# Matrix product with RMS norm on one core: roots of finished row blocks in one batch, second row factor and transpose earlier, last head copy ahead of sums

## The chip, the cores and the metric

The kernel runs on one core of a Trainium2 chip. The metric is the device time of one execution in microseconds (us), lower is better. Executions of one kernel mostly agree within 0.3%. TensorE (PE) multiplies matrices, VectorE (DVE) and ScalarE (ACT) work on elements, GpSimd (POOL) and SyncE (SP) issue transfers (DMA). A line number such as L279 is a line of the kernel. The changed kernel has more lines, so the same statement has another number there; both are given where it matters.

## The reference

```python
m, k, n = 2048, 2048, 2048          # a, b: float32, drawn from a normal distribution
x = np.matmul(a, b)
rms = np.sqrt(np.mean(x ** 2, axis=-1, keepdims=True) + eps)
return (gamma * x / rms).astype(np.float32)
```

## The kernel before

Rows of `a` are handled in 16 blocks of 128. The first four blocks (the head) are multiplied directly while `b` streams in. Blocks 4 to 15 go in pairs, called groups 2 to 7. Each group is computed in two halves of the columns, and each half with seven products of sums of quarters, in the manner of Strassen, instead of eight plain products. A product is eight 128x512 matmuls into one PSUM bank; products 4 and 3 add onto the banks of products 2 and 5, once those have been copied away or used.

A row block must be made ready for its group: ACT takes its norm (two squares and a root, `row_norm`), DVE makes a power of two of it (`row_factor`), ACT scales the block to fp16 (`row_apply`, L231), and a DMA transposes it (L186). DVE then forms sums of its quarters (`a_sums`, tiles s_103 to s_107). When a pair of rows is done, `finish` takes the root of the mean square, inverts it and multiplies the rows by it and by gamma.

```python
    def transpose_half(mb, g):
        bank = ps_t.tile([P, CH], FP32, name="tbank")
        view = bank.bitcast(FP16).rearrange("p (g m) -> p g m", m=P)
        for n in range(8):
            kt = g * 8 + n
            nc.tensor.matmul(
                view[:, n, :], a16[mb][:, kt * P:(kt + 1) * P], identity_h,
                is_transpose=True, start=(n == 0), stop=(n == 7),
            )
        nc.vector.tensor_copy(out=at(mb)[:, g * 8:(g + 1) * 8, :], in_=view)

    def transpose_dma(mb):
        nc.sync.dma_start_transpose(at(mb), a16[mb])
...
    def row_norm(mb):

        n2 = stat_pool.tile([P, 2], FP32, name="n2")
        for h in range(2):
            junk = sq_pool.tile([P, 2 * CH], BF16, name="sq")
            nc.scalar.activation(out=junk, in_=a32[mb][:, h * HALF:(h + 1) * HALF],
                                 func=ACTF.Square, scale=2.0 ** -8, accum_out=n2[:, h:h + 1])
        norm[mb] = stat_pool.tile([P, 1], FP32, name="norm")
        nc.scalar.activation(out=norm[mb], in_=n2[:, 0:1], func=ACTF.Sqrt, bias=n2[:, 1:2],
                             scale=1.0)

    def row_factor(mb):
        s = stat_pool.tile([P, 1], FP32, name="s")
        nc.vector.tensor_scalar_max(out=s, in0=norm.pop(mb), scalar1=1e-18)
        nc.vector.reciprocal(out=s, in_=s)
        nc.vector.tensor_single_scalar(out=s.bitcast(I32), in_=s.bitcast(I32),
                                       scalar=0x7F800000, op=ALU.bitwise_and)
        new_msq(mb)
        nc.vector.tensor_scalar(out=msq[mb][:, NCH:], in0=s, scalar1=s, scalar2=float(eps),
                                op0=ALU.mult, op1=ALU.mult)
        factor[mb] = s

    def row_apply(mb):
        a16[mb] = a16_slot(mb)
        if mb < HB + 2:
            nc.vector.tensor_scalar_mul(out=a16[mb], in0=a32.pop(mb), scalar1=factor.pop(mb))
        else:
            nc.scalar.activation(out=a16[mb], in_=a32.pop(mb), func=ACTF.Copy,
                                 scale=factor.pop(mb))
...
    def inverse_rms(last, partial=None):

        rms = stat_pool.tile([P, 1], FP32, name="rms")
        if partial is None:
            tot = stat_pool.tile([P, 1], FP32, name="tot")
            nc.vector.reduce_sum(out=tot, in_=msq.pop(last), axis=mybir.AxisListType.X)
            nc.scalar.activation(out=rms, in_=tot, func=ACTF.Sqrt)
        else:
            nc.scalar.activation(out=rms, in_=last, func=ACTF.Sqrt, bias=partial, scale=1.0)
        r = stat_pool.tile([P, 1], FP32, name="r")
        nc.vector.reciprocal(out=r, in_=rms)
        return r

    def rows(mb, lo, hi):
        return out[mb * P:(mb + 1) * P, lo:hi]

    def finish(mb, order=(0, 1)):
        r = inverse_rms(mb)
        for h in order:
            x = x_half.pop((mb, h))
            nc.vector.scalar_tensor_tensor(
                out=x, in0=x, scalar=r, in1=gamma_sb[:, h * HALF:(h + 1) * HALF],
                op0=ALU.mult, op1=ALU.mult)
            nc.sync.dma_start(out=rows(mb, h * HALF, (h + 1) * HALF), in_=x)
```

The end of the head, where block 5 (HB + 1) is transposed by TensorE through the one bank of `ps_t`:

```python
    groups2 = [(r, c) for r in range(HB) for c in (2, 3)][:-1]
    for kp in range(KP):
        load_later(1)
        before = [lambda: transpose_half(HB, 0)] if kp == 6 else []
        if kp == 7:
            before = [lambda: transpose_half(HB, 1)]
        stream(groups2, kp, before)
        square(squares[kp][0], x_chunk(*squares[kp]))
        if kp == 4:
            prepare(HB)
        if kp == 6:

            prepare(HB + 1)
        else:
            b_sums_2(min(kp, KP - 2))
...
    evict(groups2[2:-1], ())
    bank = new_bank()
    for kt in range(KT):
        if kt in (0, 6):
            transpose_half(HB + 1, kt // 6)
        head_matmul(bank, r3, 3, kt)
    evict(groups2[-1:], ())
    row_norm(HB + 2)
    a_sums(G0, (2, 5, 1))
    finish(0, (1, 0))
    b_sums_2(KP - 1)
    nc.scalar.copy(out=x_chunk(r3, 3), in_=bank)
    squares2(1)

```

One half of a group, and what is hooked between its products (group G0 is 2, r3 is block 3):

```python
        x11, x12, x21, x22 = (x_chunk(ra, c1), x_chunk(ra, c2), x_chunk(rb, c1), x_chunk(rb, c2))
        t = x22
        at_hook(0)
        p2, p5 = new_bank(), new_bank()
        product(g, j, 2, p2)

        c = spare if (g, j) == (G0, 0) else t
        nc.scalar.copy(out=c, in_=p2)
        last_squares()
        at_hook(1)
        product(g, j, 5, p5)
        nc.vector.tensor_tensor(out=t, in0=p5, in1=c, op=ALU.add)
        at_hook(2)
        p1 = new_bank()
        product(g, j, 1, p1)
        nc.vector.tensor_tensor(out=t, in0=p1, in1=t, op=ALU.subtract)
        at_hook(3)
        product(g, j, 4, p2, start=False)
        nc.scalar.copy(out=x21, in_=p2)
        square(rb, x21)
        nc.vector.tensor_tensor(out=x11, in0=t, in1=x21, op=ALU.add)
        at_hook(4)
        product(g, j, 3, p5, start=False)
        nc.scalar.copy(out=x12, in_=p5)
...
            else:
                if g == G0 + 1:
                    hook(2, finish, r3)
                hook(0, row_factor, nxt)
                hook(1, apply, nxt)
                hook(1, row_norm, nxt + 1)
                hook(3, row_factor, nxt + 1)
                hook(4 if g == G0 + 1 else 3, finish, 2 * g - 2)
                hook(4, apply, nxt + 1)
        else:
            if g == G0:
                hook(1, squares2, r3)
                for kp in range(KP):
                    hook(2, b_sum_6, 1, kp)
            else:
                hook(2, finish, 2 * g - 1)
            if more:
                hook(3, a_sums, g + 1, (2, 5, 1))
                hook(6, a_sums, g + 1, (7,))
                hook(7, a_sums, g + 1, (6,))
            if g + 2 < NG:
                hook(0, load_after, g, nxt + 2)
                hook(0, load_block, nxt + 3)
                hook(5, row_norm, nxt + 2)
```

In the traces here ACT, DVE and SP run their instructions in the order in which the program emits them: in the kernel before, ACT takes the norm of block 9 at 103.01 us and only then, at 103.21, the root of block 3, as the text has them. So a statement's place in this text decides what it can be held up by.

## Time and profile before

| | before |
|---|---|
| time, median of 3 runs | 226.4 us (226.37 to 226.68) |
| span of the profiled execution | 224.8 us |
| TensorE busy / DVE / ACT | 94% / 72% / 58% |
| spacing of 128x512 matmuls, start to start | 216 ns |
| time TensorE lost between 64 us and its last matmul | 0.71 + 0.53 + 1.12 = 2.36 us |

The busy share of TensorE alone says little. The Trainium skill, page "Perfetto Trace Analysis", section "Identifying the Most-Contended Engine", says that matmul busy time is no good measure of the distance to the limit, and section "Optimization Strategy" says to find the gaps of the engine and what each waits for.

These are lines of the waits view of the kernel before, filtered to TensorE. The columns are engine, tile and line, what it waited for, and then us in total, times, and longest.

```profile
PE acc L279 <- DVE s_104 L244: 1.0, 1, 1.0
PE tbank L179 <- DVE at_even L183: 0.5, 1, 0.5
PE acc L279 <- ACT x_102 L484: 0.4, 1, 0.4
```

The timeline of TensorE of the kernel before shows the same three places. The columns are start in us, duration in us, engine, line, operation, output and inputs, shape, count, and in brackets the idle time before it and what ended it.

```profile
66.25 0.59 PE L341 MATMUL acc<-b_2_87,head_at 128*128 128x512 bf16 x2
67.39 0.61 PE L179 MATMUL tbank<-identity_h,x_102 128*128 128x128 f16 x8 [0.55 <-DVE at_even L183]
...
109.70 1.89 PE L279 MATMUL acc<-early,s_103 128*128 128x512 bf16 x8
111.96 3.61 PE L279 MATMUL acc<-early,head_at 128*128 128x512 bf16 x16 [0.36 <-ACT x_102 L484]
...
118.64 0.38 PE L279 MATMUL acc<-b_7_92,s_106 128*128 128x512 bf16 x1
119.98 0.39 PE L279 MATMUL acc<-b_0_77,s_104 128*128 128x512 bf16 x1 [0.96 <-DVE s_104 L244]
```

The idle time in brackets understates the loss. A matmul's record is 0.38 us long, but its successor normally starts after 0.216 us. From start to start, the last wait is 119.98 - 118.64 = 1.34 us instead of 0.22, so 1.12 us are lost. In the same way the other two lose 0.71 and 0.53 us (each 0.16 us more than the bracket).

What stands behind the first wait is seen in DVE's timeline of the kernel before, where the copy that empties the transpose bank (L183, at 66.65) comes after the sums of slice 6 (L269, L254 and L259):

```profile
64.59 0.68 DVE L269 TENSOR_TENSOR b_6_83<-b_6_83 128x1024 bf16<-128x1024 bf16 x1
65.19 1.09 DVE L254 TENSOR_TENSOR early<-b_6_91 128x512 bf16<-128x512 bf16 x3
66.31 0.42 DVE L259 TENSOR_TENSOR b_6_91<-b_6_91 128x512 bf16<-128x512 bf16 x1
66.65 0.68 DVE L183 COPY at_even<-tbank 128x1024 f16<-128x1024 f16 x1
```

The other two waits go back to group 3, which prepares block 9. These are lines of DVE's timeline of the kernel before:

```profile
98.90 0.15 DVE L316 TENSOR_REDUCE tot<-msq 128x1 f32<-128x5 f32 x1
103.43 0.16 DVE L321 RECIPROCAL r<-rms 128x1 f32<-128x1 f32 x1 [4.38 <-ACT rms L317]
103.63 1.28 DVE L331 SCALAR_TENSOR_TENSOR x_98<-x_98,r,gamma_sb 128x1024 f32<-128x1024 f32 x1
...
107.92 0.15 DVE L316 TENSOR_REDUCE tot<-msq 128x1 f32<-128x5 f32 x1
...
119.23 0.69 DVE L244 TENSOR_TENSOR s_104<-at_even 128x1024 f16<-128x1024 f16 x1 [1.96 <-DMA at_even<-head_at]
```

And these are lines of ACT's and of SP's timelines of the kernel before in the same stretch:

```profile
103.01 0.30 ACT L212 ACTIVATE norm<-n_994 128x1 f32<-128x1 f32 x1
103.21 0.19 ACT L317 ACTIVATE rms<-tot 128x1 f32<-128x1 f32 x1
...
108.11 0.20 ACT L317 ACTIVATE rms<-tot 128x1 f32<-128x1 f32 x1 [3.48 <-DVE tot L316]
108.22 1.99 ACT L231 ACTIVATE head_at<-a_867,s 128x2048 f16<-128x2048 f32 x1
...
111.34 0.56 ACT L484 COPY x_102<-acc 128x512 f32<-128x512 f32 x1
```

```profile
111.05 0.33 SPq L334 DMA_DIRECT2D out_dram<-x_96  x1
111.48 3.35 SPq L186 DMA_TRANSPOSE at_even<-head_at  x1
```

Read together: DVE reduced the squares of block 3 at 98.90, then stood for 4.38 us until ACT took the root at 103.21, because that root stands behind the norm of block 9 in ACT's order. The root of block 4 waits 3.48 us for its sum (108.11), the scaling of block 9 stands behind that root (108.22), the copy of product 2 (L484) behind the scaling, and the transpose (111.48) behind the stores of block 4. The transpose lands at 119.2, and TensorE stands for s_104.

### The profile page before, as it was taken

Reading aid. Unit: us, or ns where it says so; the run is one execution under the profiler, and the core shown is the slowest. Engines: PE = TensorE matmul, PEld = TensorE weight load, DVE = VectorE, ACT = ScalarE, POOL = GpSimd, SP = SyncE. Lnnn points to the kernel's source line nnn. Section 1 sums busy time; section 2 is a strip of 40 time slices with the busy share of each in tenths; the row PEclk is TensorE's granted clock in tenths of the full one; section 3 lists DMA queues with packets and bytes.
Section 4 is the critical chain, followed back from the end, with each engine's and each line's share of the span. In section 5 each row is a group of like instructions: output and inputs, shape, how many; then the busy total and the mean of one; then the engine's idle time right before and its main releaser. Section 6 shows DMA issues by size and latency. Waiting matters only on the chain.

```text
span 224.8 us, 3025 instructions
## 1 busy us (share of the span) xinstructions
PE 212.1 (94%) x1043; PEld 98.6 (44%) x1043; DVE 161.8 (72%) x324; ACT 129.4 (58%) x272; POOL 24.5 (11%) x49
## 2 busy tenths in 40 slices
PE   7899999999999999999998999999999999999950
PEld 2445444444444444444443444444444444444430
DVE  1427567983998989965977578957895579687692
ACT  2210003708697895795673987698587874334570
POOL 8524232200000002000020002000200000000000
PEclk9999999999999999999999999999999999999996
DMA  6999999999962499906589369956994694044045
GB/s 190 219 203 209 202 209 210 212 305 284 331 261 117 187 280 280 345 32 169 238 210 391 118 157 241 350 205 169 225 337 187 96 279 187 0 187 191 0 188 187
DMA packets 36176, 47.13 MB, mean 210 GB/s; under 512 B 21952, under 2 KB 26048, under 8 KB 34496
## 3 DMA queue, kind: packets, MB, share of 16 engines
q0 software_dynamic: 9648, 23.33, 41.3%
q1 hardware_dynamic: 26080, 22.29, 32.7%
q10 hardware_dynamic: 432, 1.31, 2.0%
q8 instruction: 8, 0.13, 0.2%
q14 instruction: 8, 0.07, 0.1%
HBM read 34.60 MB, written 16.78 MB: 229 GB/s over the span
## 4 chain that ended last, share of the span: by engine, by line
PE 57%; DMA 14%; issue 12%; DVE 6%; ACT 5%; POOL 3%; DVEq 0%; ACTq 0%; POOLq 0%
PE acc L279 41%; PE acc L341 15%; DMA b_4_81<-in_b_dram 8%; DMA at_even<-head_at 3%; DMA a_865<-in_a_dram 2%; ACT sq L209 2%; ACT sq L291 1%; POOL early L106 1%; ACT head_at L231 1%; PE tbank L373 1%; PE tbank L165 1%; DVE x_95 L331 1%; DVE x_98 L331 1%; DVE x_96 L331 1%; DVE x_102 L331 1%
## 5 line engine op out<-in xcount | busy, mean ns | idle before, releaser
L341 PEld LDWEIGHTS <-head_at 128*128 128x128 bf16 x240 | 22.9, 98 | 26.6 <-issue 1.1
L279 PEld LDWEIGHTS <-s_104 128*128 128x128 f16 x96 | 9.3, 98 | 12.5 <-DVE s_104 L244 1.4
L279 PEld LDWEIGHTS <-head_at 128*128 128x128 f16 x96 | 9.4, 98 | 11.9 <-issue 0.6
L279 PEld LDWEIGHTS <-s_105 128*128 128x128 f16 x96 | 9.4, 98 | 11.3
L279 PEld LDWEIGHTS <-s_103 128*128 128x128 f16 x96 | 9.4, 98 | 11.3
L279 PEld LDWEIGHTS <-at_even 128*128 128x128 f16 x96 | 9.4, 98 | 11.3
L279 PEld LDWEIGHTS <-s_107 128*128 128x128 f16 x96 | 9.4, 98 | 11.3
L384 ACT COPY x_95<-acc 128x512 f32<-128x512 f32 x1 | 0.6, 585 | 23.8 <-PE acc L341 23.8
L279 PEld LDWEIGHTS <-s_106 128*128 128x128 f16 x88 | 8.6, 98 | 10.4
L279 PE MATMUL acc<-t_left,s_103 128*128 128x512 bf16 x48 | 11.3, 379 | 0.0
L279 PE MATMUL acc<-early,s_103 128*128 128x512 bf16 x48 | 11.3, 379 | 0.0
L279 PE MATMUL acc<-early,head_at 128*128 128x512 bf16 x48 | 10.8, 379 | 0.4 <-ACT x_102 L484 0.4
L279 PE MATMUL acc<-early,at_even 128*128 128x512 bf16 x48 | 10.8, 379 | 0.0
L279 PE MATMUL acc<-t_left,at_even 128*128 128x512 bf16 x48 | 10.8, 379 | 0.0
L279 PE MATMUL acc<-t_left,head_at 128*128 128x512 bf16 x48 | 10.8, 379 | 0.0
L379 DVE TENSOR_TENSOR x_98<-tbank,x_98 128x512 f32<-128x512 f32 x7 | 4.8, 692 | 7.6 <-PE tbank L373 7.6
L317 ACT ACTIVATE rms<-tot 128x1 f32<-128x1 f32 x14 | 2.8, 199 | 12.2 <-DVE tot L316 12.2
L217 DVE TENSOR_SCALAR s<-norm 128x1 f32<-128x1 f32 x12 | 1.8, 148 | 10.9 <-ACT norm L212 10.9
L321 DVE RECIPROCAL r<-rms 128x1 f32<-128x1 f32 x16 | 2.6, 164 | 9.5 <-ACT rms L317 8.4
L170 DVE COPY head_at<-tbank 128x1024 bf16<-128x1024 bf16 x7 | 4.8, 692 | 6.2 <-PE tbank L165 6.2
L291 ACT ACTIVATE sq<-x_97 128x512 bf16<-128x512 f32 x8 | 5.0, 628 | 3.5 <-DVE x_97 L599 3.0
L209 ACT ACTIVATE sq<-a_430 128x1024 bf16<-128x1024 f32 x2 | 2.1, 1058 | 7.5 <-DMA a_430<-in_a_dram 7.5
(390 smaller groups left out, 552.6 us busy)
## 6 DMA issues: line engine op xcount, KB each, us to landing
out_dram<-x_99 SPq DMA_DIRECT2D x4, 512.0 KB, 3.5
out_dram<-x_95 SPq DMA_DIRECT2D x4, 512.0 KB, 2.6
out_dram<-x_96 SPq DMA_DIRECT2D x4, 512.0 KB, 3.0
out_dram<-x_100 SPq DMA_DIRECT2D x4, 512.0 KB, 6.0
out_dram<-x_97 SPq DMA_DIRECT2D x4, 512.0 KB, 2.8
out_dram<-x_101 SPq DMA_DIRECT2D x4, 512.0 KB, 3.7
early<-in_a_dram POOLq DMA_DIRECT2D x7, 256.0 KB, 15.2
out_dram<-x_98 SPq DMA_DIRECT2D x3, 512.0 KB, 2.7
```

Source lines behind the costliest of these rows:

```text
L106: nc.gpsimd.dma_start(out=ah(kp), in_=a[0:HB * P, kp * W2:(kp + 1) * W2].rearrange("(r p) k -> p r k", p=P))
L165: nc.tensor.matmul(view[:, t, r, :], ah(kp)[:, r, t * P:(t + 1) * P], identity, is_transpose=True, start=(t == 0 and r == 0), stop=(t == 1 ...
L170: nc.vector.tensor_copy(out=head_at[:, 2 * kp:2 * kp + 2, :, :], in_=view)
L209: nc.scalar.activation(out=junk, in_=a32[mb][:, h * HALF:(h + 1) * HALF], func=ACTF.Square, scale=2.0 ** -8, accum_out=n2[:, h:h + 1])
L231: nc.scalar.activation(out=a16[mb], in_=a32.pop(mb), func=ACTF.Copy, scale=factor.pop(mb))
L279: nc.tensor.matmul(bank, lhsT[:, kp, :], rhs, start=(start and kp == 0), stop=(kp == KP - 1), skip_group_check=not start)
L291: nc.scalar.activation(out=sq[:, 0:CH], in_=src, func=ACTF.Square, scale=inv_sqrt_n, accum_out=msq[mb][:, c:c + 1])
L317: nc.scalar.activation(out=rms, in_=tot, func=ACTF.Sqrt)
L321: nc.vector.reciprocal(out=r, in_=rms)
L331: nc.vector.scalar_tensor_tensor(out=x, in0=x, scalar=r, in1=gamma_sb[:, h * HALF:(h + 1) * HALF], op0=ALU.mult, op1=ALU.mult)
L341: nc.tensor.matmul(bank, head_at[:, kt, r, :], head_rhs(c, kt), start=(kt == 0), stop=(kt == KT - 1))
L379: nc.vector.tensor_tensor(out=x, in0=part, in1=x, op=ALU.add)
```

## The change

It means to shorten these waits by order alone. The roots of all finished blocks are taken in one batch before the next block's norm (`take_rms`); the second row factor comes earlier, meant to let its scaling and transpose start earlier too; and at the end of the head the copy out of the transpose bank goes ahead of the sums of slice 6 (of L254 and L259; those of L269 stay ahead of it). No instruction is added or removed.

```diff
--- before.py
+++ after.py
@@ -308,24 +308,33 @@
     def x_chunk(mb, c):
         return x_tile(mb, c // 2)[:, (c % 2) * CH:(c % 2 + 1) * CH]
 
-    def inverse_rms(last, partial=None):
-
-        rms = stat_pool.tile([P, 1], FP32, name="rms")
-        if partial is None:
-            tot = stat_pool.tile([P, 1], FP32, name="tot")
-            nc.vector.reduce_sum(out=tot, in_=msq.pop(last), axis=mybir.AxisListType.X)
-            nc.scalar.activation(out=rms, in_=tot, func=ACTF.Sqrt)
-        else:
-            nc.scalar.activation(out=rms, in_=last, func=ACTF.Sqrt, bias=partial, scale=1.0)
+    rms_of = {}
+
+    def take_rms(mb):
+
+        tot = stat_pool.tile([P, 1], FP32, name="tot")
+        nc.vector.reduce_sum(out=tot, in_=msq.pop(mb), axis=mybir.AxisListType.X)
+        rms_of[mb] = stat_pool.tile([P, 1], FP32, name="rms")
+        nc.scalar.activation(out=rms_of[mb], in_=tot, func=ACTF.Sqrt)
+
+    def inverse(rms):
         r = stat_pool.tile([P, 1], FP32, name="r")
         nc.vector.reciprocal(out=r, in_=rms)
         return r
 
+    def inverse_rms(last, partial):
+
+        rms = stat_pool.tile([P, 1], FP32, name="rms")
+        nc.scalar.activation(out=rms, in_=last, func=ACTF.Sqrt, bias=partial, scale=1.0)
+        return inverse(rms)
+
     def rows(mb, lo, hi):
         return out[mb * P:(mb + 1) * P, lo:hi]
 
     def finish(mb, order=(0, 1)):
-        r = inverse_rms(mb)
+        if mb not in rms_of:
+            take_rms(mb)
+        r = inverse(rms_of.pop(mb))
         for h in order:
             x = x_half.pop((mb, h))
             nc.vector.scalar_tensor_tensor(
@@ -431,8 +440,10 @@
         if kp == 6:
 
             prepare(HB + 1)
+        elif kp == KP - 1:
+            b_sums_in_place(0, kp - 1)
         else:
-            b_sums_2(min(kp, KP - 2))
+            b_sums_2(kp)
     nc.gpsimd.dma_start(out=gamma_sb, in_=gamma.partition_broadcast(P))
     load_block(HB + 2)
     load_block(HB + 3)
@@ -449,6 +460,9 @@
     for kt in range(KT):
         if kt in (0, 6):
             transpose_half(HB + 1, kt // 6)
+            if kt == 0:
+                b_sums(1, KP - 2)
+                b_sum_7(1, KP - 2)
         head_matmul(bank, r3, 3, kt)
     evict(groups2[-1:], ())
     row_norm(HB + 2)
@@ -545,12 +559,16 @@
                 hook(4, finish, 2)
                 hook(6, b_sum_7, 1, KP - 1)
             else:
+                done = [2 * g - 2, 2 * g - 1]
+                hook(0, row_factor, nxt)
+                hook(1, apply, nxt)
                 if g == G0 + 1:
                     hook(2, finish, r3)
-                hook(0, row_factor, nxt)
-                hook(1, apply, nxt)
+                    done.insert(0, r3)
+                for mb in done:
+                    hook(1, take_rms, mb)
                 hook(1, row_norm, nxt + 1)
-                hook(3, row_factor, nxt + 1)
+                hook(2, row_factor, nxt + 1)
                 hook(4 if g == G0 + 1 else 3, finish, 2 * g - 2)
                 hook(4, apply, nxt + 1)
         else:
```

## The prediction

> **What bounds the kernel now.** TensorE. In PE's timeline, from 25 us to the last product, 128x512 matmuls follow each other every 216 ns, except in three places (926, 741 and 1335 ns from start to start), which lose:
> - 0.71 us at 67.4: the last head transposes wait for the one transpose bank, whose copy (DVE L183) stands behind the sums of slice 6 (1.09 + 0.42 us).
> - 0.53 us at 112.0 (group 3, half 1): product 4 adds onto product 2's bank and waits for ACT's copy of it (L484 at 111.34), though product 2 ended near 108. ACT is late because the scaling L231 of block 9 started only at 108.2, behind a root (L317) that waited 3.5 us for DVE.
> - 1.12 us at 120.0: the first product of group 4 waits for s_104, that for the DMA transpose of block 9, issued at 111.48, landed at 119.2.
>
> Together 2.36 us. From group 4 on PE shows no wait. The start and the tail after the last matmul (8 us) aren't touched.
>
> **What the change does.** It adds no work; only orders move.
> 1. Head copy ahead of the sums: the bank is free near 66.3, before PE's next transposes at 66.7. The 0.71 us go. The second half's copy starts only 0.4 us earlier while PE comes 0.7 earlier: s_104 is ready about 0.15 us before its need, and product 5's first add frees its bank just when product 3 needs it. I allow 0.1 us.
> 2. Three roots (0.1 to 0.2 us each) before block 9's norm: ACT's squares start 0.3 us later, but DVE no longer waits 4.4 us for the root (idle before L321 at 103.4); the finish of r3 (2.5 us) fills that hole.
> 3. Row factor two products earlier, with that finish out of its way: done near 104.4 instead of 107.4. ACT scales block 9 near 104.8 instead of 108.2, then copies product 2 near 108.4, 2.5 us before its need: the 0.53 us go. The transpose stands on SP behind block 4's stores, so it is issued near 108.7 (2.8 us earlier) and lands near 116.4 if it takes its 7.7 us again. s_104 is ready near 117.1, 1 us before PE needs it: the 1.12 us go.
> 4. Groups 4 to 6: the same moves where PE does not wait. Norms come 0.1 to 0.4 us later, the subtraction of product 1 (L492) 4 to 5 us later, but its bank isn't needed until then. No gain.
>
> Batching roots saves no table switch. The Trainium skill, "ScalarE: Activation LUTs", section "What ACT_TABLE_LOAD costs", gives 1283 ns for a load; the trace agrees (1283 ns), but has only two, both before 55 us.
>
> **Predicted time.** 226.4 - 2.36 + 0.1 = 224.1 us; 223.8 to 225.2 should hold it 8 times in 10. Faster by over 2%: 0.01; within 2%: 0.98; slower by over 2%: 0.01.
>
> **What would show each step.** In PE's waits: L179 on the copy, and L279 on ACT L484 and on s_104, gone or under 0.1 us. In the timelines: the first L183 copy of block 5 near 65.6; three roots in a row near 100; block 9's L231 near 104; its transpose issued near 108, landed near 115.7 (0.7 less for step 1's shift); PE's last matmul near 214.5 instead of 216.8. Still two table loads.
>
> **What would make it wrong.** Block 9's transpose meets the earlier loads of blocks 10 and 11 and takes over 9 us: up to 1 us of the third wait returns. The batched sums hold back product 5's add (L502 after) in group 4, whose margin before product 3 was 0.7 us. Step 1's margins in group 2 may be short by some tenths.

## The result, and the profile after

| | before | after |
|---|---|---|
| time, median | 226.54 us (226.37 to 226.69, 4 runs) | 224.50 us (224.26 to 224.63, 4 runs) |
| span of the profiled execution | 224.8 us | 222.6 us |
| time TensorE lost from 64 us on | 2.36 us | 0.06 + 0.16 = 0.21 us |

The ratio is 0.9909, with a 95% interval of 0.9892 to 0.9926.

The waits view of TensorE after, complete:

```profile
PE acc L138 <- DVE sq L129: 1.5, 1, 1.5
PE tbank L148 <- POOL msq L198: 1.2, 1, 1.2
PE acc L350 <- DMA b<-in_b_dram: 0.4, 1, 0.4
PE tbank L382 <- DVE head_at L170: 0.4, 1, 0.4
```

All four are in the first 25 us, at the start of the head. In this document "after the start" means from 64 us on. The three of before are gone. DVE's timeline of the changed kernel at the end of the head and in group 3 (L322 and L340 are L321 and L331 of before):

```profile
65.55 0.69 DVE L183 COPY at_even<-tbank 128x1024 f16<-128x1024 f16 x1 [0.43 <-PE tbank L179]
66.16 1.09 DVE L254 TENSOR_TENSOR early<-b 128x512 bf16<-128x512 bf16 x3
...
100.46 0.16 DVE L322 RECIPROCAL r<-rms 128x1 f32<-128x1 f32 x1 [1.21 <-ACT rms L318]
100.66 2.48 DVE L340 SCALAR_TENSOR_TENSOR x<-x,r,gamma_sb 128x1024 f32<-128x1024 f32 x2
103.19 0.15 DVE L217 TENSOR_SCALAR s<-norm 128x1 f32<-128x1 f32 x1
...
116.41 1.89 DVE L244 TENSOR_TENSOR s<-at_even 128x1024 f16<-128x1024 f16 x3 [2.79 <-DMA at_even<-head_at]
```

ACT's and SP's timelines of the changed kernel in the same stretch (L318 is the root, L498 the copy of product 2):

```profile
100.23 0.37 ACT L318 ACTIVATE rms<-tot 128x1 f32<-128x1 f32 x3
...
104.30 1.99 ACT L231 ACTIVATE head_at<-a,s 128x2048 f16<-128x2048 f32 x1
...
107.64 0.59 ACT L498 COPY x<-acc 128x512 f32<-128x512 f32 x1
```

```profile
108.41 3.40 SPq L186 DMA_TRANSPOSE at_even<-head_at  x1
```

The three roots stand in a row at 100.23 and take 0.37 us together. The Trainium skill, page "ScalarE: Activation LUTs", section "What ACT_TABLE_LOAD costs", gives 186 ns plus 0.83 ns per element for an activation with immediate scale and bias, and says that neighbours overlap by about 93 ns; if that is what these roots are, three take 187 + 2 x 94 = 375 ns by an estimate from these figures, and the trace agrees (0.37 us). DVE's hole shrank from 4.38 to 1.21 us, block 9 is scaled 3.9 us earlier and its transpose issued 3.1 us earlier. It took 8.0 us to land (116.4), and s_104 was ready at 117.1, about 0.7 us before TensorE needed it at 117.8 (product 7 of that half started at 114.35, and 16 matmuls take 3.45 us).

Two waits are new, and small. Sixteen unhindered matmuls of products 4 and 3 take 3.62 us in this view. The timeline of TensorE in group 2 after, half 0 and half 1:

```profile
74.43 3.67 PE L279 MATMUL acc<-t_left,at_even 128*128 128x512 bf16 x16
...
86.57 3.77 PE L279 MATMUL acc<-early,at_even 128*128 128x512 bf16 x16
```

From start to start, product 3 comes 0.06 us late in half 0 and 0.16 us late in half 1. In both it waits for DVE's first add of product 5 (L502 after, L488 before), which ends 0.05 us before it starts.

### The profile page after: what moved, and what is told of

It reads as the page before. It is cut to its first block, busy times and chain, and to the rows that moved or that the text cites. A ratio compares the mean times of both kernels' runs of the same rounds, so it can differ in the third digit from the quotient of the medians.

```text
span 222.6 us, 3026 instructions
## 1 busy us (share of the span) xinstructions
PE 211.1 (95%) x1043; PEld 98.6 (44%) x1043; DVE 161.8 (73%) x324; ACT 129.1 (58%) x272; POOL 24.5 (11%) x49
## 4 chain that ended last, share of the span: by engine, by line
PE 83%; DMA 8%; DVE 2%; POOL 2%; issue 1%; ACT 1%; DVEq 0%; ACTq 0%; POOLq 0%
PE acc L279 63%; PE acc L350 18%; DMA b<-in_b_dram 8%; POOL early L106 1%; DVE x L617 1%; POOL b L100 1%; DVE x L620 1%; PE tbank L179 1%; PE tbank L382 1%; PE tbank L165 1%; ACT sq L291 0%; DVEq L732 0%; ACT sq L682 0%; DVE x L690 0%; DVE r L322 0%
## 5 line engine op out<-in xcount | busy, mean ns | idle before, releaser
L279 PE MATMUL acc<-b,s 128*128 128x512 bf16 x376 | 83.3, 379 | 0.0
L279 PEld LDWEIGHTS <-s 128*128 128x128 f16 x472 | 46.2, 98 | 55.7 <-DVE s L244 0.2
L350 PE MATMUL acc<-b,head_at 128*128 128x512 bf16 x240 | 55.1, 379 | 0.6 <-DMA b<-in_b_dram 0.4
L291 ACT ACTIVATE sq<-x 128x512 bf16<-128x512 f32 x62 | 39.1, 631 | 10.9 <-DVE x L520 5.1
L340 DVE SCALAR_TENSOR_TENSOR x<-x,r,gamma_sb 128x1024 f32<-128x1024 f32 x28 | 34.7, 1282 | 0.8
L209 ACT ACTIVATE sq<-a 128x1024 bf16<-128x1024 f32 x24 | 25.4, 1057 | 16.8 <-DMA a<-in_a_dram 16.4
L393 ACT COPY x<-acc 128x512 f32<-128x512 f32 x11 | 5.9, 591 | 25.1 <-PE acc L350 25.1
L231 ACT ACTIVATE head_at<-a,s 128x2048 f16<-128x2048 f32 x10 | 19.9, 1990 | 0.0
L291 ACT ACTIVATION_READ_ACCUMULATOR sq<-x 128x1 f32 x62 | 11.7, 188 | 0.0
L279 PE MATMUL acc<-t_left,s 128*128 128x512 bf16 x48 | 11.3, 379 | 0.0
L509 ACT COPY x<-acc 128x512 f32<-128x512 f32 x10 | 5.7, 575 | 8.9 <-PE acc L279 8.9
```

What stands on the lines that cost most here:

```text
L279: nc.tensor.matmul(bank, lhsT[:, kp, :], rhs, start=(start and kp == 0), stop=(kp == KP - 1), skip_group_check=not start)
L291: nc.scalar.activation(out=sq[:, 0:CH], in_=src, func=ACTF.Square, scale=inv_sqrt_n, accum_out=msq[mb][:, c:c + 1])
L340: nc.vector.scalar_tensor_tensor(out=x, in0=x, scalar=r, in1=gamma_sb[:, h * HALF:(h + 1) * HALF], op0=ALU.mult, op1=ALU.mult)
L350: nc.tensor.matmul(bank, head_at[:, kt, r, :], head_rhs(c, kt), start=(kt == 0), stop=(kt == KT - 1))
L393: copy(out=x_chunk(*g), in_=banks[g])
```

## The experiments

The theory was this. TensorE sets the time, so the gain is the three lost times less what is newly lost. The two later waits have one root cause, DVE's hole before the root of block 3. Rivals were that the parts need each other, that the earlier row factor is what gets the transpose out, that the order of root, scaling and stores of block 4 was the whole cause, and that the batches in groups 4 to 6 carry part of it. Each kernel was timed in five rounds against the kernel before, four kernels to a chip. All gave correct results.

### 1. The head copy alone

```diff
+        elif kp == KP - 1:
+            b_sums_in_place(0, kp - 1)
         else:
-            b_sums_2(min(kp, KP - 2))
+            b_sums_2(kp)
...
             transpose_half(HB + 1, kt // 6)
+            if kt == 0:
+                b_sums(1, KP - 2)
+                b_sum_7(1, KP - 2)
```

> The kernel before with the head copy move alone. Theory (three separate waits of TensorE add up to the gain): the wait of the last head transposes (0.71 us) is gone, the waits of product 4 in group 3 (0.53 us) and on s_104 in group 4 (1.12 us) stay at 0.5 to 0.7 and 1.0 to 1.3 us, and the two small new waits of group 2 (0.06 and 0.16 us before product 3) show as in the changed kernel. Net gain 0.45 to 0.5 us: ratio 0.998. Rival (most of the gain comes from the whole chain being earlier, the head copy moving everything): ratio 0.994 or less, and the later waits shrink with it.

Measured: 226.05 us (225.89 to 226.72, 6 runs), ratio 0.9983 (0.9969 to 0.9997). The gain was about as expected, 0.4 us by the ratio and 0.5 us by the medians. In the profiled execution the wait of the head transposes is gone and the two small waits of group 2 are there, as expected. But the two later waits were longer than expected. The timeline of TensorE of this kernel, lines with a wait in group 3 and at the start of group 4:

```profile
111.90 3.61 PE L279 MATMUL acc<-early,head_at 128*128 128x512 bf16 x16 [0.75 <-ACT x L489]
120.14 1.04 PE L279 MATMUL acc<-b,s 128*128 128x512 bf16 x4 [1.17 <-DVE s L244]
```

Both starts (111.90 and 120.14) are nearly those of the kernel before (111.96 and 119.98). TensorE came earlier and stood longer there: 0.75 and 1.17 us against 0.36 and 0.96. So in this execution all that the head copy won was taken back by the start of group 4: TensorE lost 2.45 us in all, against 2.36 before. ACT started on block 8, when its load had landed, at 94.31 us, almost as in the kernel before (94.36). But the profiled execution was one of the two longest of six (226.72 and 226.66). The other four took 225.89 to 226.06, 0.5 to 0.6 us less than the median of the kernel before (226.52), which is about the 0.71 - 0.06 - 0.16 = 0.49 us of the theory. So it is not shown that the later waits grow in those too. The rival, that this move carries most of the gain, fell.

### 2. The groups' new order alone

The changed kernel with the lines of experiment 1 taken back.

> The changed kernel with the head copy put back behind the sums. Theory: the wait of the last head transposes is back (0.71 us), the waits of 0.53 and 1.12 us are gone, and group 2 shows no new small waits, since the vector engine and TensorE are both late by the same. Net gain 1.6 us: ratio 0.993. Rival (the parts need each other): gain well below 1.6 us.

Measured: 224.91 us (224.62 to 224.97, 5 runs), ratio 0.9927 (0.9915 to 0.9939), so a gain of 1.65 us as expected. The profile shows the wait of the head transposes (0.71 us from start to start) and no other wait after the start. Gains of experiments 1 and 2 add up to that of the whole change (0.39 + 1.65 = 2.04 of 2.06 us by the ratios).

### 3. The roots without the row factor, and the row factor without the roots

Roots only, starting from experiment 2:

```diff
-                hook(2, row_factor, nxt + 1)
+                hook(3, row_factor, nxt + 1)
```

> The batch of roots alone: no head copy move, and the second row factor stays at product 4's place. Theory (the root ahead of the norm is what frees the vector engine; the factor follows at nearly the same time, since the finish of r3 fills the hole and ends when the norm does): as the kernel with both, gain 1.6 us, ratio 0.993; block 9's transpose is issued within 0.5 us of the changed kernel's. Rival (the earlier row factor gets the transpose out): gain below 0.5 us, ratio 0.998 or more.

The row factor only, starting from the kernel before:

```diff
-                hook(3, row_factor, nxt + 1)
+                hook(2, row_factor, nxt + 1)
```

> The earlier row factor alone, roots as before. Theory: the factor stands behind the finish of r3, whose root still comes after block 9's norm, so it is done only 0.6 us earlier, and ACT's scaling of block 9 still stands behind the root of block 4, which waits for the vector engine: no gain, ratio 0.999 to 1.001, both later waits of TensorE stay near 0.5 and 1.1 us. Rival (the earlier row factor is what gets the transpose out): gain 1.6 us, ratio 0.993.

Measured: roots only 224.57 us (224.54 to 224.76, 4 runs), ratio 0.9917 (0.9904 to 0.9930). Row factor only 226.79 us (226.71 to 227.21, 5 runs), ratio 1.0017 (1.0005 to 1.0029). DVE's timelines show the root of block 3 used at 100.24 us in the kernel with the roots only, and at 103.43 in the one with the row factor only:

```profile
100.24 0.16 DVE L322 RECIPROCAL r<-rms 128x1 f32<-128x1 f32 x1 [1.22 <-ACT rms L318]
```

```profile
103.43 0.17 DVE L321 RECIPROCAL r<-rms 128x1 f32<-128x1 f32 x1 [4.28 <-ACT rms L317]
```

In the first, block 9's transpose is issued at 107.85 us, 0.6 us before that of the changed kernel (within 0.5 us was expected); its two waits are gone. In the second it is issued at 111.66 us, later than before, and all three waits are there, the last one larger (1.59 us lost, against 1.12). So the roots carry the whole gain of the groups, and the earlier row factor none. Why the row factor alone costs 0.4 us rather than nothing was not pursued; the profiled execution was the longest of its five, and 0.2 us of its longer waits are at the head, which this edit doesn't touch.

### 4. Only a swap in group 3

```diff
+                if g == G0 + 1:
+                    hook(4, apply, nxt + 1)
                 hook(4 if g == G0 + 1 else 3, finish, 2 * g - 2)
-                hook(4, apply, nxt + 1)
+                if g != G0 + 1:
+                    hook(4, apply, nxt + 1)
```

> The kernel before with one swap in group 3: block 9 is scaled and transposed before block 4 is finished, so neither the root nor the stores of block 4 stand ahead of it; nothing else moves. Theory (what the change won is the vector engine's 4.4 us hole before the root of r3; moving the transpose alone does not fill it): the transpose is issued about 2 us earlier (near 109.4) and the waits of product 4 and on s_104 go, but the finish of block 4 comes 1.2 us later, the add of product 5 in half 1 with it, and product 3 of that half waits 1 to 1.5 us for it: net between 0.3 us faster and 1 us slower, ratio 0.999 to 1.005. Rival (the root and the stores ahead of block 9 were the whole cause): gain 1.6 us, ratio 0.993, no wait at product 3.

Measured: 225.87 us (225.75 to 226.77, 6 runs), ratio 0.9979 (0.9961 to 0.9997), that is 0.5 us faster, a little more than the best expected. The two waits are gone, and the expected new one is there. The timeline of TensorE of this kernel:

```profile
111.26 1.89 PE L279 MATMUL acc<-early,head_at 128*128 128x512 bf16 x8
114.19 1.89 PE L279 MATMUL acc<-early,head_at 128*128 128x512 bf16 x8 [1.04 <-DVE x L488]
```

Product 3 stood 1.2 us from start to start (114.19 - 111.26 - 8 x 0.216) for the add of product 5. DVE's hole before the root of block 3 was still 4.30 us. Letting the transpose pass the stores only moves DVE's lateness to the next thing that TensorE needs from DVE.

### 5. The new order in group 3 alone

The changed kernel, with groups 4 to 6 in the old order; the changed kernel itself ran beside it.

> The changed kernel with its new order in group 3 alone; groups 4 to 6 have the old order. Theory: TensorE never waits in groups 4 to 6 either way, so as the changed kernel: ratio 0.991, within 0.1 us of the run of the changed kernel beside it. Rival (the batches of groups 4 to 6 carry a part of the gain): ratio 0.994 or more, with waits of TensorE in groups 4 to 6.

> The changed kernel itself again, as the yardstick on this chip: ratio 0.991, two small waits before product 3 in group 2 (0.06 and 0.16 us) and none later.

Measured: group 3 alone 224.26 us (224.05 to 224.71, 6 runs), ratio 0.9902 (0.9886 to 0.9919). The changed kernel again 224.36 us (224.25 to 224.68, 5 runs), ratio 0.9909 (0.9893 to 0.9924). They are the same within noise, and their profiles show the same two small waits in group 2 and none later. The new order in groups 4 to 6 does nothing.

### 6. The two small new waits

```diff
     evict(groups2[2:-1], ())
+    take_rms(0)
```

> The changed kernel with the root of block 0 taken before the last head transposes, where the vector engine has 0.4 us to spare. Theory (the two small new waits come from the vector engine's chain in group 2, which is 0.4 us earlier than before while TensorE is 0.7 us earlier): the chain from the finish of block 0 on is 0.4 us earlier, both waits before product 3 in group 2 go: 0.2 us faster than the changed kernel, ratio 0.990. Rival (those waits have another cause): as the changed kernel.

Measured: 224.04 us (223.99 to 224.45, 5 runs), ratio 0.9897 (0.9880 to 0.9913). The medians differ by 0.3 us from the changed kernel beside it, but the intervals overlap, so the time alone doesn't prove it. The profile does: both waits before product 3 are gone, and no matmul from 64 us to the last starts late. DVE's timeline of this kernel shows the root used without a wait; in the changed kernel the same reciprocal waited 0.27 us for the root, at 70.58.

```profile
64.82 0.15 DVE L316 TENSOR_REDUCE tot<-msq 128x1 f32<-128x5 f32 x1
65.35 0.69 DVE L183 COPY at_even<-tbank 128x1024 f16<-128x1024 f16 x1 [0.38 <-PE tbank L179]
...
69.95 0.15 DVE L322 RECIPROCAL r<-rms 128x1 f32<-128x1 f32 x1
```

### 7. How little is enough

Three more kernels asked whether the batch is needed at all, with the kernel of experiment 6 run again as the yardstick. One is that kernel with the late row factor. One is the kernel before with a single root moved. One has the head copy, the root of block 0 and the root of block 3 moved, and nothing else. The edit of the last two is the same, made in the kernel of experiment 2 for the one root and in that of experiment 6 for the two; with an empty list, group 3 still puts block 3 in.

```diff
-                done = [2 * g - 2, 2 * g - 1]
+                done = []
-                hook(2, row_factor, nxt + 1)
+                hook(3, row_factor, nxt + 1)
```

> The kernel with the root of block 0 early, its second row factors put back to product 4's place. Theory (the row factor's move is worth nothing once the root of r3 is early): ratio 0.990, within 0.15 us of the same kernel with the early factor beside it, no wait of TensorE after the start. Rival (the factor's move counts): 0.3 us or more slower, with a wait on s_104 or on the copy of product 2.

> The kernel before with one single root moved: that of r3, ahead of block 9's norm in group 3. No other root, no row factor, no head copy moves. Theory (this one root opens the 4.4 us hole of the vector engine, and everything later in group 3 follows): both later waits of TensorE gone, the wait of the head transposes stays: gain 1.6 us, ratio 0.993 to 0.992, as the whole batch gave. Rival (the batch is needed, since block 4's root still stands ahead of block 9's scaling): gain below 1 us, ratio over 0.9955.

> The kernel before with three small moves: the head copy ahead of the sums, the root of block 0 ahead of the last head transposes, and the root of r3 ahead of block 9's norm; groups 4 to 6 as before. Theory: all waits of TensorE after the start are gone: ratio 0.990, the same as the kernel with all roots batched and the root of block 0 early.

> The changed kernel with the root of block 0 early, again, as the yardstick on this chip: ratio 0.990, no wait of TensorE after the start.

| kernel | median us | runs from, to | ratio (95%) |
|---|---|---|---|
| early root, late factor | 224.23 | 224.05, 224.40 (4) | 0.9892 (0.9873 to 0.9911) |
| one root moved | 224.65 | 224.43, 224.68 (4) | 0.9908 (0.9890 to 0.9926) |
| head copy and two roots moved | 224.03 | 223.97, 224.20 (4) | 0.9884 (0.9866 to 0.9902) |
| early root, all batches (again) | 224.27 | 224.06, 224.52 (4) | 0.9893 (0.9870 to 0.9916) |

One moved root gives the whole gain of the groups. The waits view of TensorE of that kernel, complete, shows the wait of the head transposes as the only one after the start:

```profile
PE acc L138 <- DVE sq L129: 1.5, 1, 1.5
PE tbank L179 <- DVE at_even L183: 0.5, 1, 0.5
PE tbank L382 <- DVE head_at L170: 0.4, 1, 0.4
PE tbank L148 <- POOL msq L198: 0.2, 1, 0.2
```

Block 4's root still stands ahead of block 9's scaling there, yet it costs only a short wait now. ACT's timeline of that kernel, the line that answers to the 3.48 us of before, and DVE's, the line that answers to the 4.38 us:

```profile
105.69 0.20 ACT L318 ACTIVATE rms<-tot 128x1 f32<-128x1 f32 x1 [0.94 <-DVE tot L316]
```

```profile
101.01 0.16 DVE L322 RECIPROCAL r<-rms 128x1 f32<-128x1 f32 x1 [2.25 <-ACT rms L318]
```

DVE's hole isn't closed, only about halved: the root now stands ahead of block 9's norm, but still behind the scaling of block 8 (98.90 to 100.89 us). That was enough.

The kernel with the head copy and two roots moved is as fast as any that was run, and the simplest. It has no wait of TensorE after the start. It was run at another time. Its lead over the changed kernel (0.3 to 0.5 us by the medians) is not well known.

### The sum over all profiles

If TensorE alone sets the time, the time less what TensorE lost from 64 us on should be one number for all kernels. Lost time is from start to start, over 216 ns. In the last four traces (those of experiment 7) 20 of the 1043 matmul records are missing, one every 50 or so; the double spacing that each leaves is not counted as lost.

| kernel | time of the profiled run, us | lost, us | difference, us |
|---|---|---|---|
| before | 226.6 | 2.36 | 224.2 |
| after | 224.4 | 0.21 | 224.2 |
| head copy alone | 226.72 | 2.45 | 224.3 |
| groups alone | 224.91 | 0.71 | 224.2 |
| roots only | 224.54 | 0.49 | 224.1 |
| row factor only | 227.21 | 3.15 | 224.1 |
| swap | 225.95 | 1.80 | 224.2 |
| group 3 alone | 224.44 | 0.20 | 224.2 |
| after, again | 224.32 | 0.20 | 224.1 |
| one root | 224.68 | 0.66 | 224.0 |
| early root / two roots | 223.99 / 223.97 | 0 / 0 | 224.0 / 224.0 |
| late factor / early root again | 224.36 / 224.36 | 0 / 0 | 224.4 / 224.4 |

It is, within 0.2 us of 224.2, in all fourteen. The 224.2 is read off these same kernels, so the table tests only that time and loss rise together. The rest lies before 64 us or after the last matmul, where no kernel here differs by intent, and was not followed. A late start near 61 us, of 0.03 to 0.32 us, is in five of the fourteen (head copy alone, row factor only, group 3 alone, late factor, early root again).

## Why the prediction was right or wrong

The time, 224.5 us, lies in the stated range, and the class (within 2%) was right.

- **The three waits and their size** were right. 2.36 us were lost before, and all three waits went. The copy came at 65.55 (65.6 predicted), the roots at 100.2 (near 100), the scaling of block 9 at 104.30 (near 104), the transpose at 108.4 (near 108), PE's last matmul at 214.4 (near 214.5), and the trace has two table loads, as before.
- **The allowance of 0.1 us** was the mis-sized term. The new small waits took 0.06 and 0.16 us. The first was named ("product 5's first add frees its bank just when product 3 needs it"); the second, in half 1 of the same group, where DVE's chain is just as late, was overlooked. Experiment 6 shows where they come from.
- **The transpose** took 8.0 us, not 7.7, and landed at 116.4, not 115.7. The margin at s_104 was 0.7 us, not 1. It was enough.
- **Step 3 gave the credit to the wrong part.** "Row factor two products earlier, with that finish out of its way" is right only in its second half. The edit moves the row factor past one product, not two. Experiments 3 and 7 show that its place is worth nothing, and that the other roots of the batch aren't needed: the single root of block 3 removes both waits. What counts is step 2, the early root that frees DVE. The time alone couldn't tell, since the moves that count and those that don't came in one edit.
- **Step 1's 0.71 us** are gone in the whole change. Alone, the head copy is worth about 0.4 us (0.1 to 0.7 by the interval), which fits 0.71 less the two new small waits. In one profiled execution the next two waits grew when TensorE came earlier and took all of it back (experiment 1); whether they do so as a rule is not shown. The gains of experiments 1 and 2 do add up to that of the whole, as the prediction's sum has it.
- **Groups 4 to 6: no gain.** Right (experiment 5).
- **The rest.** The measured 224.5 us is 0.4 us above 224.1. About 0.1 us of it is the allowance, and 0.14 us is in the base: in the rounds of the result, the kernel before took 226.54 us, not 226.40, so the gain was 2.04 us against 2.3 predicted. What is left, under 0.2 us, is less than the spread of the runs (224.26 to 224.63).

## What to carry to other kernels

When one engine is busy nearly all of the time, list its late starts from start to start, follow each back over the engines, and add up; in twelve kernels the time less that sum was one number to 0.2 us. A tiny instruction on an in-order engine can hold a whole chain: here a root of 0.2 us, queued behind a norm (100.67 to 103.31 us) and a scaling, kept DVE idle for 4.4 us, and moving that one root ahead of the norm was worth as much as the whole reordering of the groups. Test each move of such a change alone, since waits that look separate can share a cause: here two of the three had one, and the move that was credited with them was worth nothing.

## What the Trainium skill lacked or had wrong

- "TensorE: Matmul & The Clock Gate", section "Back-to-back issue gap", gives about 131 ns per matmul of 512 columns in a stream of weight load and matmul pairs, and calls 216 ns the isolated gap. Here every matmul has its weight load (1043 of each), and the spacing over stretches of hundreds of matmuls is 216 ns at the granted clock of 1.00 that the windows view shows; the 215.7 ns of the same page's section "Step-by-step: what each phase is for" is what the runs agree with.
- "DMA: Bandwidth & Descriptors", section "DMA Transpose (X-bar)", gives constraints but no duration, and the page's figure for its speed, in another section, is a bandwidth and no time from issue to landing. A 128x2048 fp16 block from SBUF to SBUF landed 4.6 to 5.0 us after its issue in the median of the kernel before. Block 9's, issued right behind block 4's stores, took 7.7 us before and 8.0 us after, and 4.3 us in the kernel of experiment 4 (108.96 to 113.23), where those stores came behind it. The issue held SP for 1.7 to 3.4 us.
- "ScalarE: Activation LUTs" doesn't give the cost of reading the accumulator: each activation with a summed output is followed by a read of 188 ns in the mean (in the changed kernel 62 of them after squares of 512 columns, 11.7 us).
